# Operand tiles 64 bytes longer, read and written from 16 bytes past their start

## The chip, the cores and the metric

The kernel runs on one core of a Trainium2 chip. The metric is the device time of one execution in microseconds (us), the median of several runs; lower is better. A profile of one execution goes with it.

## What is computed

A two-layer encoder over 512 tokens of width 1024: layer 0 mixes tokens by neighbourhood attention (16 heads of 64), layer 1 by latent attention (low-rank queries and keys/values, 16 heads of 96). Each mixer's input projection also gives a SiLU gate; after each layer comes a sigmoid gate times an embedding projection.

```python
for i in range(DEPTH):                       # DEPTH = 2
    xn = rmsnorm(x, norm_g[i])
    if i % 2 == 0: y = mixer_na(xn, na_w_in[j], na_rpb[j], na_w_out[j])
    else:          y = mixer_mla(xn, mla_w_in[j], ..., mla_w_out[j])
    h = x + y
    gate = jax.nn.sigmoid(rmsnorm(h, ple_norm[i]) @ ple_w_gate[i])
    x = h + gate * (p[i] @ ple_w_proj[i])
return rmsnorm(x, final_norm)
# both mixers: (attention(...) * silu(z)) @ w_out
```

## The kernel before

Everything is float32 in memory. TensorE multiplies in a reduced float32 form (`float32r`), so each operand is kept as two tiles, a rounded part `hi` and the rest `lo`, and each product is the sum of three matmuls: hi by hi, lo by hi, hi by lo. A weight tile arrives by DMA in `wraw`; ScalarE copies it to `hi` (line 83, or 583 in the gate phases), and GpSimd, sometimes VectorE, subtracts to make `lo` (line 84 or 585). Activations are transposed on TensorE into PSUM and split the same way, by ScalarE (94) and VectorE (96), into "big" tiles of 128 partitions by four blocks of 512 elements.

The program runs through these stages: the layer-0 embedding projection and the first gates, the neighbourhood heads (projections at line 107, scores at 351 and 352, outputs at 400), the output projection, the gate matmul by seven block products (`gate_seven`, matmuls at 637), then the latent projections (`mla_c`), the latent heads (scores at 107, queries, keys and values at 734 and 107, outputs at 845), and the same tail again. A scheduler fixes the order of instructions on every engine when the program is built; `issue_after` pins some of them.

Two kinds of tile matter here. **Big tiles** come from `bigtile`, a pool of eight buffers of 8,192 bytes a partition; they hold the turned inputs (`x`, `x1`, `r`), the attention outputs (`o`, `o1`), the probabilities of the latent heads (`pt_hi`, `pt_lo`) and the blocks `X` of the gate matmul. **Weight tiles** `whi` and `wlo` (`w4` where more are kept) come from `load_w`, `gate_seven` and the start of `run`, mostly 4,096 bytes a partition. Not among them are the raw weights, the operands of the first embedding projection, the score operands of both kinds of head (`sa`, `da`, `qe`, `ke` and the like), the compressed latents `cT`, the values `vt` and the transposes' inputs.

In the built program before, all 2,916 matmuls on `float32r` read both operands from 32 bytes past a multiple of 64. The 488 transposes of data read the data from such a place too and the identity from a multiple of 64; the other 15 matmuls are the warm-up on a constant and four turns of a column of scales.

Of the kernel before, what the change touches and what calls it, by code (L numbers as in the profile page):

```python
# [13 lines left out]
F32 = mybir.dt.float32  # L14
F32R = mybir.dt.float32r
# [4 lines left out]
P = 128  # L20
S = 512
# [8 lines left out]
NLATE = 3  # L30
NEARLY = 7
SEVEN = (0, 1)


def win(t, r0, r1, off, dims):
# [5 lines left out]
class Trunk:  # L41
# [20 lines left out]
        self.sums = [{p: dram.tile([2 * P, D], F32, name=f"sum{l}{p}") for p in (4, 5, 6, 7)} for l in range(2)]  # L62

    def bigtile(self, name):
        return self.big.tile([P, 4, S], F32R, name=name, tag="big")

    def psum(self, tag, shape=(P, S)):
        t = self.ps.tile([P, S], F32, name="ps_" + tag, tag=tag, bufs={"mm": 2, "S": 2, "T": 3, "O": 1}[tag])
# [3 lines left out]
    def load_w(self, ap, n, extra=False, parts=1, rest=None, late=None):  # L72

        nc = self.nc
        pool = self.wx if extra else self.wp
        raw = self.wp.tile([P, 1024], F32, name="wraw", tag="wraw", bufs=3)
        tags = ("w4", "w4") if extra and self.wxn > 5 else ("whi", "wlo")
        hi, lo = (pool.tile([P, n if extra else 1024], F32R, name="whi"[:1] + t, tag=t, bufs=self.wxn if extra else 3)
                  for t in tags)
        w = n // parts  # L80
        for c in [slice(i * w, (i + 1) * w) for i in range(parts)]:
            self.last_load = nc.sync.dma_start(raw[:, c], ap[:, c])
            nc.scalar.activation(hi[:, c], raw[:, c], AF.Copy)  # L83
            f = lambda e, c=c: e.tensor_tensor(out=lo[:, c], in0=raw[:, c], in1=hi[:, c].bitcast(F32), op=ALU.subtract)  # L84
            if late is not None and c.stop == n:
                late.append(lambda: f(nc.gpsimd))
            else:
                f(rest or nc.gpsimd)
        return hi, lo
# [474 lines left out]
    def gate_seven(self, pool, layer, rh, res, after):  # L564
# [6 lines left out]
        def prep(p, after=None):  # L571
            nonlocal pieces
            W[p] = []
            src = self.quarter[layer][p] if p < 4 else self.sums[layer][p]
            for c in range(2):
                own = pieces % turns < 3
                pieces += 1
                raw = self.wp.tile([P, 1024], F32, name="wraw", tag="wraw", bufs=3)
                q, n = (self.wp, 3) if own else (pool, self.wxn)
                hi, lo = (q.tile([P, 1024], F32R, name=t, tag=t if own else "w4", bufs=n) for t in ("whi", "wlo"))  # L580
                nc.sync.dma_start(raw, src[c * P:(c + 1) * P])
                with self.tc.issue_after(after.ins) if after else nullcontext():
                    nc.scalar.activation(hi, raw, AF.Copy)  # L583
                for o in (slice(0, S), slice(S, 2 * S)):
                    nc.gpsimd.tensor_tensor(out=lo[:, o], in0=raw[:, o], in1=hi[:, o].bitcast(F32), op=ALU.subtract)  # L585
                W[p].append((hi, lo))
# [23 lines left out]
        for p in order[:4]:  # L610
            prep(p)
# [7 lines left out]
        for k, p in enumerate(order):  # L619
            if k in (1, 2):  # L620
                prep(order[k + 3])
# [5 lines left out]
            for i in range(2):  # L627
                for o, wd in halves if i and p in (7, 4) else ((0, S),):
# [26 lines left out]
                    elif p == 5:  # L655
                        q = self.psum("mm" if i else "T")
# [287 lines left out]
    def run(self):  # L944
        tc, nc, a = self.tc, self.nc, self.a
        def pair(n):
            return [self.bigtile(f"{n}h{g}") for g in range(2)], [self.bigtile(f"{n}l{g}") for g in range(2)]
# [4 lines left out]
        with tc.tile_pool(name="pre", bufs=4, reuse_waits="tile") as pool:  # L952
            ones = [nc.const_aps.tensor(1.0, (P, n), mybir.dt.bfloat16) for n in (P, S)]
            ps = self.psum("T")
            for i in range(NWARM):
                nc.tensor.matmul(ps, *ones, start=True, stop=True)
            operands = self.ple_load(0, pool)
            g0 = pool.tile([P, KD], F32, name="g0", bufs=1)
            nc.sync.dma_start(g0, a["g0"])

            raw, xT = pair("r"), pair("x")
            part = lambda T, k: [T[s][k // 4][:, k % 4, :] for s in range(2)]
            xs = [pool.tile([P, S], F32, name="xT", tag="xT", bufs=8) for k in range(KD)]
            ws = [[self.wp.tile([P, 1024], d, name=n, tag=n, bufs=3)
                   for n, d in (("wraw", F32), ("whi", F32R), ("wlo", F32R))] for _ in range(3)]
            first = ws.pop()
            for h in range(2):
                for k in range(4 * h, 4 * h + 4):
                    nc.sync.dma_start(xs[k], a["xT"][k])
                    hi, lo = part(raw, k)  # L970
                    nc.scalar.activation(hi, xs[k], AF.Copy, scale=g0[:, k:k + 1])
                    nc.vector.scalar_tensor_tensor(lo, xs[k], g0[:, k:k + 1], hi.bitcast(F32), op0=ALU.mult,
                                                   op1=ALU.subtract)
                for j in range(2):
                    wr, hi, lo = (x[:, h * S:(h + 1) * S] for x in ws[j])
                    nc.sync.dma_start(wr, a["na_z"][j][:, h * S:(h + 1) * S])
                    nc.scalar.activation(hi, wr, AF.Copy)
                    nc.vector.tensor_tensor(out=lo, in0=wr, in1=hi.bitcast(F32), op=ALU.subtract)
            ws = [w[1:] for w in ws]
            nc.sync.dma_start(self.ident, a["ident"])  # L980
            ss = pool.tile([P, NT], F32, name="ssq", bufs=1)
            xt = [pool.tile([P, D], F32, name="x", tag="x", bufs=4) for t in range(NT)]
            for t in range(NT):
                if t == 2:
                    nc.sync.dma_start(first[0], a["na_z"][2])
                nc.sync.dma_start(xt[t], a["x"][t])
                nc.scalar.activation(xt[t], xt[t], AF.Square, accum_out=ss[:, t:t + 1])
            self.ple(pool, 0, "pe", 6, operands)
            nc.gpsimd.tensor_scalar(ss, ss, 1.0 / D, EPS, op0=ALU.mult, op1=ALU.add)
            nc.gpsimd.tensor_scalar(self.rows[0][0], ss, 1.0, None, op0=ALU.add)  # L990
            nc.gpsimd.tensor_tensor(out=ss, in0=ss, in1=self.half.to_broadcast([P, NT]), op=ALU.pow)
            turned = self.transposes([ss[:, t:t + 1].to_broadcast([P, P]) for t in range(NT)])
            R = pool.tile([P, S], F32, name="R", bufs=1)
            nc.scalar.activation(first[1], first[0], AF.Copy)
            nc.gpsimd.tensor_tensor(out=first[2], in0=first[0], in1=first[1].bitcast(F32), op=ALU.subtract)
            nc.scalar.activation(R, turned, AF.Copy)
            zs = self.z_phase(a["na_z"], raw, range(2), R=R, ws=ws)
            for k in range(KD):
                hi, lo = part(xT, k)
                nc.vector.scalar_tensor_tensor(xs[k], turned, g0[:, k:k + 1], xs[k], op0=ALU.mult, op1=ALU.mult)  # L1000
                nc.scalar.activation(hi, xs[k], AF.Copy)
                (nc.vector, nc.gpsimd)[k % 2].tensor_tensor(out=lo, in0=xs[k], in1=hi.bitcast(F32), op=ALU.subtract)
            zs.update(self.z_phase(a["na_z"], raw, range(2, 8 - NLATE), R=R, first=first[1:]))
# [5 lines left out]
        for layer in range(2):  # L1009
            with tc.tile_pool(name=f"out{layer}", bufs=4, reuse_waits="tile") as pool:  # L1010
                seven = layer in SEVEN
                self.wx, self.wxn = pool, 10 if seven else 5
# [207 lines left out]
```

## Time and profile before

| | |
|---|---|
| median of 3 runs | 661.67 us (661.35 to 662.09) |
| the profiled execution | 660.85 us, of which its span is 658.7 us |
| TensorE matmuls | 647.8 us busy, 98% of the span |
| weight loads (beside the matmuls) | 550.8 us, 84% |
| VectorE, ScalarE, GpSimd | 61%, 67%, 66% of the span |
| granted TensorE clock, mean | 0.996 |

A matmul's "busy" time overlaps with the next one's, because matmuls are pipelined: one of 512 columns is shown as about 390 ns, while the next one starts some 227 ns later. So the pace is read from the chain of work that ended last, which gives the time that a run of matmuls took and how many they were, and not from the mean of one.

### The profile page before, as it was taken

Reading aid. Unit: us, or ns where it says so; the run is one execution under the profiler, and the core shown is the slowest. Engines: PE = TensorE matmul, PEld = TensorE weight load, DVE = VectorE, ACT = ScalarE, POOL = GpSimd, SP = SyncE. Lnnn points to the kernel's source line nnn. Section 1 sums busy time; section 2 is a strip of 40 time slices with the busy share of each in tenths; the row PEclk is TensorE's granted clock in tenths of the full one; section 3 lists DMA queues with packets and bytes.
Section 4 is the critical chain, followed back from the end, with each engine's and each line's share of the span. In section 5 each row is a group of like instructions: output and inputs, shape, how many; then the busy total and the mean of one; then the engine's idle time right before and its main releaser. Section 6 shows DMA issues by size and latency. Waiting matters only on the chain.

```text
span 658.7 us, 10121 instructions
## 1 busy us (share of the span) xinstructions
PE 647.8 (98%) x3419; PEld 550.8 (84%) x3419; DVE 403.7 (61%) x856; ACT 439.2 (67%) x875; POOL 432.8 (66%) x381
## 2 busy tenths in 40 slices
PE   9999999999999999999999999999999999999994
PEld 6888888988988888887899888888888888888884
DVE  6280365836646516568834613888888876474865
ACT  7672586757767743787543635887979897537945
POOL 0495485696686573787555525785959878436974
PEclk9999999999999999999999999999999999999998
DMA  9944256886577869445733334120111213583524
GB/s 328 346 149 142 97 169 186 231 203 160 166 212 175 223 166 348 158 149 162 247 85 118 103 102 148 54 77 6 63 53 65 66 65 128 200 312 128 168 89 159
DMA packets 44755, 102.18 MB, mean 155 GB/s; under 512 B 4640, under 2 KB 17696, under 8 KB 44704
## 3 DMA queue, kind: packets, MB, share of 16 engines
q1 hardware_dynamic: 33776, 83.97, 37.8%
q0 software_dynamic: 10496, 16.78, 11.7%
q10 hardware_dynamic: 432, 0.79, 0.3%
q8 instruction: 27, 0.44, 0.3%
q14 instruction: 24, 0.20, 0.1%
HBM read 89.99 MB, written 25.17 MB: 175 GB/s over the span
## 4 chain that ended last, share of the span: by engine, by line
PE 91%; DVE 2%; ACT 2%; POOL 2%; issue 1%; DMA 1%; POOLq 0%; ACTq 0%
PE ps_mm L107 35%; PE ps_S L107 13%; PE ps_mm L734 6%; PE ps_T L139 5%; PE ps_O L845 4%; PE ps_T L637 4%; PE ps_T L107 3%; PE ps_O L107 3%; PE ps_T L238 2%; PE ps_O L400 2%; PE ps_S L637 2%; PE ps_mm L637 2%; PE ps_mm L184 2%; PE ps_T L388 2%; PE ps_S L352 1%
## 5 line engine op out<-in xcount | busy, mean ns | idle before, releaser
L84 POOL TENSOR_TENSOR wwlo<-wraw,wwhi 128x1024 fp32r<-128x1024 f32 (+5 forms) x78 | 142.7, 1842 | 72.8 <-ACT wwhi L83 51.9
L83 ACT ACTIVATE wwhi<-wraw 128x1024 fp32r<-128x1024 f32 (+5 forms) x81 | 65.5, 832 | 54.5 <-issue 21.0
L585 POOL TENSOR_TENSOR wlo<-wraw,whi 128x512 fp32r<-128x512 f32 x56 | 73.9, 1352 | 24.2 <-ACT whi L583 19.3
L830 POOL TENSOR_TENSOR ex<-ex,rc 128x512 f32<-128x512 f32 x64 | 65.9, 1037 | 25.2 <-DVE rc L829 18.1
L828 ACT ACTIVATE ex<-ps_S,mx 128x512 f32<-128x512 f32 x64 | 44.0, 687 | 12.1 <-DVE mx L826 11.0
L826 DVE TENSOR_REDUCE mx<-ps_S 128x1 f32<-128x512 f32 x64 | 43.7, 682 | 7.1 <-PE ps_S L107 6.7
L96 DVE TENSOR_TENSOR pt_lo<-ps_T,pt_hi 128x512 fp32r<-128x512 f32 x64 | 43.3, 682 | 7.7 <-ACT pt_hi L94 7.3
L374 POOL TENSOR_TENSOR ex<-ex,rc 128x128 f32<-128x128 f32 (+1 forms) x64 | 35.7, 617 | 14.6 <-DVE rc L370 14.6
L94 ACT ACTIVATE pt_hi<-ps_T 128x512 fp32r<-128x512 f32 x64 | 37.7, 595 | 4.3 <-PE ps_T L139 4.1
L107 PE MATMUL ps_mm<-xh,wwhi 128*128 128x512 f32 x152 | 40.3, 398 | 0.0
L107 PE MATMUL ps_mm<-xl,wwhi 128*128 128x512 f32 x152 | 38.5, 391 | 0.0
L139 PE MATMUL ps_T<-ident,ex 128*128 128x128 f32 x256 | 38.4, 272 | 0.0
L107 PE MATMUL ps_mm<-xh,wwlo 128*128 128x512 f32 x152 | 38.2, 392 | 0.0
L139 PEld LDWEIGHTS ps_T<-ident,ex 128*128 128x128 f32 x256 | 31.5, 140 | 7.7 <-POOL ex L830 0.4
L107 PEld LDWEIGHTS ps_mm<-xh,wwlo 128*128 128x128 f32 x152 | 28.3, 188 | 5.9
L107 PEld LDWEIGHTS ps_mm<-xl,wwhi 128*128 128x128 f32 x152 | 28.4, 188 | 5.7
L583 ACT ACTIVATE whi<-wraw 128x1024 fp32r<-128x1024 f32 x28 | 29.2, 1055 | 5.1 <-DMA wraw<-sum 3.0
L205 DVE TENSOR_TENSOR u<-ps_O,u 64x512 f32<-64x512 f32 x32 | 22.0, 686 | 17.2 <-ACT u L204 16.7
L209 POOL TENSOR_TENSOR u<-u,z 128x512 f32<-128x512 f32 x16 | 21.8, 1360 | 16.0 <-DVE u L205 9.1
L368 ACT ACTIVATE ex<-ex,mx 128x128 f32<-128x128 f32 (+1 forms) x64 | 30.3, 475 | 1.9 <-DVE mx L358 1.1
L107 PEld LDWEIGHTS ps_mm<-xh,wwhi 128*128 128x128 f32 x152 | 27.3, 189 | 4.7
L107 PE MATMUL ps_S<-ke,qe 96*128 96x512 f32 x96 | 29.1, 408 | 0.3 <-DMA qe<-rl 0.3
(432 smaller groups left out, 1848.8 us busy)
## 6 DMA issues: line engine op xcount, KB each, us to landing
sum<-gate POOLq DMA_DIRECT2D x12, 1024.0 KB, 7.8
wraw<-na_qk SPq DMA_DIRECT2D x16, 512.0 KB, 3.3
wraw<-sum SPq DMA_DIRECT2D x16, 512.0 KB, 3.3
pe<-pe SPq DMA_DIRECT2D x31, 256.0 KB, 6.9
wraw<-gate SPq DMA_DIRECT2D x12, 512.0 KB, 3.4
wraw<-na_v SPq DMA_DIRECT2D x8, 512.0 KB, 4.2
sum<-sum POOLq DMA_DIRECT2D x4, 1024.0 KB, 9.0
wraw<-na_o SPq DMA_DIRECT2D x8, 512.0 KB, 3.6
```

What stands on the lines that cost most here:

```text
L83: nc.scalar.activation(hi[:, c], raw[:, c], AF.Copy)
L84: f = lambda e, c=c: e.tensor_tensor(out=lo[:, c], in0=raw[:, c], in1=hi[:, c].bitcast(F32), op=ALU.subtract)
L94: self.last_copy = nc.scalar.activation(hi, src, AF.Copy, scale=scale)
L96: nc.vector.tensor_tensor(out=lo, in0=src, in1=hi.bitcast(F32), op=ALU.subtract)
L107: last = self.last_mm = nc.tensor.matmul(out, l, r, start=i == 0, stop=i == n - 1)
L139: self.last_mm = self.nc.tensor.transpose(t[:, i * P:(i + 1) * P], b, self.ident)
L585: nc.gpsimd.tensor_tensor(out=lo[:, o], in0=raw[:, o], in1=hi[:, o].bitcast(F32), op=ALU.subtract)
L637: mm = nc.tensor.matmul(ps, l, r, start=j == 0 and p in banks, stop=j == 11 and p in (2, 3, 4), skip_group_check=True)
L734: self.last_mm = nc.tensor.matmul(PS[key], *terms[i], start=i == 0, stop=i == len(terms) - 1)
L826: nc.vector.reduce_max(mx, sp, axis=AX.X, negate=True)
L828: nc.scalar.activation(ex, sp, AF.Exp, bias=mx, accum_out=sm)
L830: nc.gpsimd.tensor_tensor(out=ex, in0=ex, in1=rc.to_broadcast([P, S]), op=ALU.mult)
```

## The change

Each of the tiles named above is allocated 16 elements (64 bytes) longer, and only the elements from the fifth on (16 bytes in) are used. `skewed` does both. It is called for big tiles, for the weight tiles of `load_w`, of `gate_seven` and of the start of `run`.

```diff
+GAP = 16
+BEGIN = 4
@@ bigtile
-        return self.big.tile([P, 4, S], F32R, name=name, tag="big")
+        return self.skewed(self.big, 4 * S, F32R, name, "big", 8).rearrange("p (a b) -> p a b", a=4)
+
+    def skewed(self, pool, n, d, name, tag, bufs, begin=BEGIN):
+        return pool.tile([P, n + GAP], d, name=name, tag=tag, bufs=bufs)[:, begin:begin + n]
@@ load_w
-        hi, lo = (pool.tile([P, n if extra else 1024], F32R, name="whi"[:1] + t, tag=t, bufs=self.wxn if extra else 3)
+        hi, lo = (self.skewed(pool, n if extra else 1024, F32R, "whi"[:1] + t, t, self.wxn if extra else 3)
                   for t in tags)
@@ gate_seven, prep
-                hi, lo = (q.tile([P, 1024], F32R, name=t, tag=t if own else "w4", bufs=n) for t in ("whi", "wlo"))
+                hi, lo = (self.skewed(q, 1024, F32R, t, t if own else "w4", n) for t in ("whi", "wlo"))
@@ run
-            ws = [[self.wp.tile([P, 1024], d, name=n, tag=n, bufs=3)
-                   for n, d in (("wraw", F32), ("whi", F32R), ("wlo", F32R))] for _ in range(3)]
+            ws = [[self.wp.tile([P, 1024], F32, name="wraw", tag="wraw", bufs=3),
+                   *(self.skewed(self.wp, 1024, F32R, n, n, 3) for n in ("whi", "wlo"))] for _ in range(3)]
```

In the built program the instructions of all five engines stand in the same order as before, with the same shapes. What differs is addresses. The tiles named start 48 bytes past a multiple of 64 where they started at 32. Before, all of them started at the same place of a stretch of 512 bytes (416); now neighbours in a pool differ by 64. Tiles behind these pools are pushed up by 64 bytes per buffer ahead of them and keep their place within 64. Of the 3,419 matmuls, 2,420 read at least one such tile: 1,892 of 512 columns, 336 of 256, 96 of 384 and 96 of 288. So do, reading or writing, 256 instructions of ScalarE, 159 of GpSimd and 125 of VectorE. Because buffers that were freed are covered by other tiles than before, ten instructions wait for other semaphores (four on VectorE, one on ScalarE, five DMAs of SyncE); one of them, a VectorE subtraction of the second output projection, now also waits for GpSimd, and two VectorE multiplies there no longer do.

## The prediction

> **What bounds the kernel now.** I read the page's busy times first, then its chain of work that ended last, then that chain in order of time, for the pace of single stretches.
>
> ```profile
> span 658.7 us, 10121 instructions
> PE 647.8 (98%) x3419; PEld 550.8 (84%) x3419; DVE 403.7 (61%) x856; ACT 439.2 (67%) x875; POOL 432.8 (66%) x381
> PEclk9999999999999999999999999999999999999998
> PE 91%; DVE 2%; ACT 2%; POOL 2%; issue 1%; DMA 1%; POOLq 0%; ACTq 0%
> ```
>
> TensorE (PE) holds 91% of the chain, and its clock is granted in full nearly everywhere. The other three engines together hold 6%, about 40 us. So this change pays or costs almost only through the pace of matmuls; what it does to ScalarE, VectorE and GpSimd counts in those 40 us alone. The chain in order of time (start, us, what) gives the pace of runs of one shape:
>
> ```profile
> 66.15 16.32 PE ps_mm L107 x72
> 333.88 4.87 PE ps_S L107 x28
> 343.94 4.24 PE ps_T L107 x32
> 425.67 0.93 PE ps_O L845 x4
> 438.97 1.44 PE ps_mm L107 x12
> ```
>
> The first run is projections of 512 columns: 16.32 / 72 = 226.7 ns each. The second is latent projections of 384 columns: 173.9 ns. The third is the same of 288 columns: 132.5. The fourth is latent-head outputs of 512 columns: 232.5. The fifth is values of 256 columns: 120. From 256 to 512 columns the pace grows by 106.7 ns, 0.417 ns a column, which leaves 226.7 - 512 x 0.417 = **13.3 ns a matmul that is not columns**. At 384 columns the same split gives 160 + 13.9, and at 288 it gives 120 + 12.5. That is the quantity at stake: a fixed piece of each matmul, present at every width, for which no engine is waited for.
>
> **Is that piece made by other engines' traffic to the tiles?** Within the first stretch the columns of the next view are: the stretch, its us, busy us of PE, weight loads, VectorE, ScalarE and GpSimd with their counts, granted clock, DMA share.
>
> ```profile
> 66.15:82.47 16.32, 16.32 (x75) 13.52 (x74) 5.87 (x14) 8.99 (x16) 7.18 (x3) 1.00 0.29 97
> 400.00:560.00 160.00, 159.67 (x867) 133.78 (x866) 129.42 (x257) 133.32 (x292) 126.91 (x116) 1.00 0.22 68
> ```
>
> In the first, GpSimd (7.18 us) and ScalarE (8.99) work for about half of the time, mostly on `lo` and `hi` tiles, and the pace is 226.7. Two later runs of the same projections, in the middle of the neighbourhood heads:
>
> ```profile
> 139.24 10.91 PE ps_mm L107 x48
> 151.27 5.49 PE ps_mm L107 x24
> ```
>
> They take 227.3 and 228.8. So what the other engines do around a projection adds a nanosecond or two, not thirteen. In the latent heads, where three engines are busy for 80% of the time, matmuls of 512 columns take about 232.5, 5.8 more; but the engines there mostly read the matmuls' own results in PSUM, which the change doesn't move.
>
> **The change, part by part.** No instruction is added, removed or moved, and no transfer grows: the raw weights land in tiles of the same size. So there are four terms.
>
> *The start of matmul operands.* 2,420 matmuls (of the built program: 1,892 of 512 columns, 336 of 256, 96 of 384, 96 of 288) read at least one tile from 16 bytes further on. Nothing in the trace has a float32r operand that starts at 48 past 64, so this has no row of its own, and I bound it. From below, the whole fixed piece goes: 2,420 x 13.3 ns = 32 us off. From above, it doubles: 32 us on. Between them, one more unit to fetch per matmul would cost what its columns cost: 16 bytes are 4 columns, 1.7 ns, in all 4 us; 32 bytes are 8 columns, 3.3 ns, 8 us. The nearest rows are the five paces. Their tiles lie at many different places beyond 512 bytes, and the 288-column weights alternate between two places within 512 (their rows are 1,152 bytes); the piece stays at 12.5 to 13.9. That looks like a price of changing weights, not of the address. I take **0**.
>
> *Neighbouring tiles no longer in step.* Before, all tiles started at one place of 512 bytes, so a collision between a weight load and the running matmul, if there is one, would be alike everywhere. Now it would vary from pair to pair. Since 384 and 512 columns pay the same piece, although the weight load is long over when the longer one ends, I take 0 here too, with the same bounds as above, not to be added to them.
>
> *Work of the other engines on these tiles.* The costliest groups, with busy us and mean ns of one:
>
> ```profile
> L84 POOL TENSOR_TENSOR wwlo<-wraw,wwhi 128x1024 fp32r<-128x1024 f32 x41 | 100.3, 2454 | 51.1 <-ACT wwhi L83 35.8 <-PE ps_O L238 7.5 <-PE ps_mm L107 7.1
> L84 POOL TENSOR_TENSOR wwlo<-wraw,wwhi 128x1024 fp32r<-128x1024 f32 x3 | 7.2, 2394 | 9.1 <-PE ps_mm L107 6.1 <-PE ps_O L238 3.1
> L84 POOL TENSOR_TENSOR ww<-wraw,ww 128x1024 fp32r<-128x1024 f32 x4 | 10.5, 2613 | 12.0 <-ACT ww L83 12.0
> L83 ACT ACTIVATE wwhi<-wraw 128x1024 fp32r<-128x1024 f32 x43 | 45.1, 1058 | 40.9 <-issue 21.0 <-PE ps_O L238 8.8 <-DMA wraw<-na_z 4.3
> L83 ACT ACTIVATE ww<-wraw 128x1024 fp32r<-128x1024 f32 x10 | 10.1, 1051 | 12.6 <-DMA wraw<-mla_o 7.1 <-DMA wraw<-na_o 5.5
> ```
>
> The second row is the quiet stretch from 66 us. The same subtraction takes 2,394 to 2,613 ns from place to place, a band of 9%; the copy 1,051 to 1,058. GpSimd's share of the chain is 2%, 13 us; 9% of it is 1.2 us. ScalarE's and VectorE's 13 us each, at the copy's band of 1%, give 0.1. Most of this work lies beside matmuls: in the first stretch GpSimd is idle for 9 of 16 us. If a subtraction were late, the matmul that reads `lo` would wait, the last third of each product; the place with no cover is the turn from output projection to gate matmul:
>
> ```profile
> 282.59 3.00 POOL wlo L585 x2
> 285.61 3.28 DMA wraw<-sum
> 288.99 1.06 ACT whi L583
> ```
>
> There 9% of 3.00 is 0.3 us. I take 0, bounds minus 1.3 and plus 1.3.
>
> *Ten changed waits.* The one that adds an engine is a VectorE subtraction of the second output projection that now follows GpSimd; queued behind it on VectorE are the sums of that projection, which the turns of `hg` and so TensorE wait for. At worst it waits out one subtraction, 2.6 us by the row above; the two multiplies that lose a wait on GpSimd could win as much. The five SyncE moves of the rotary slab keep their order and trade waits among themselves, so the last of them can go at about the same time. I take 0, bounds plus and minus 2.6.
>
> **The sum** is 0 + 0 + 0 + 0 on the profiled execution's 660.85 us (span 658.7 and 2.15 around it). The three shown runs have their median 0.8 above it, so I predict **661.7 us**. The small terms alone give plus or minus 3.9, 658 to 666.
>
> **The Trainium skill against the rows.** "SBUF — State Buffer", Specifications (TRN2), states lines of 16 bytes. By that rule a start 16 bytes on is at the start of a line again and nothing changes, which agrees with my sum; the trace has no case that tests it. "TensorE: Matmul & The Clock Gate", Back-to-back issue gap, gives columns / 2.4 plus 2.5 ns for warm matmuls, an estimate of 215.8 ns at 512 columns. The row above says 226.7, so the measurement decides on the pace; but if the 10.8 ns between them were a price of where these tiles start, they could be won: 2,420 x 10.8 = 26 us, 636 us. No run here shows which it is. It speaks for the first rival below.
>
> **The rivals.**
>
> *Operands read faster from the new places.* Part of the 13.3 ns then is a stall that comes from all tiles starting in step, or 32 past 64. For it: the piece is there at every width, with no engine waited for. Against: it doesn't vary over the many places that the trace has. Half of it would be 16 us, 646 us; all of it 630.
>
> *Operands read slower, one more unit per matmul.* A start 32 past 64 is a multiple of 32; 48 is not. If operands come in units of 32 bytes, each of the 2,420 matmuls fetches one more. The price is 8 columns each, 8 us: 670 us, on the other side from no change. It decides from about 0.6 ns a matmul (1.3 us, 0.2%). Since matmuls run back to back through 91% of the chain, nothing would hide it. Against: no row shows such a unit.
>
> *Slower by the small terms.* GpSimd's subtraction at the top of its band and the added wait: 1.3 + 2.6 = 3.9, and as likely half of it: 664 us. Faster by the same terms: 659.
>
> *The change does nothing at all* is my forecast itself, since all it does is move addresses.
>
> **How the numbers follow.** No change 0.30. Matmuls faster 0.28, the small terms faster 0.07. Matmuls slower 0.22, the small terms slower 0.13. This kernel's runs differ by 0.1%, so about 0.2% (1.3 us) can be told from no change. That makes faster 0.35, same 0.30, slower 0.35. The likeliest case's own range is 658 to 666. For 8 in 10 the range must reach into both matmul cases: down to 644, just past half of the fixed piece (what is left out below is some 0.10), up to 672, one unit of 32 bytes with the small term (some 0.10 above).
>
> **What would show it.** In the profile after, the stretch of 72 projections should still take 16.3 us, the 384-column run 4.9 and the 288-column run 4.2; the GpSimd subtraction of 1,024 should stay between 2,394 and 2,613 ns. If the 72 take 16.6 or more, the second rival holds; if 15.8 or less, the first. If the runs keep their pace and the time still moves, the waits or the stretch from 276 to 306 us have changed. The forecast is wrong if the pace of 512 columns moves by more than 0.6 ns.

## The result, and the profile after

The kernel with the change takes 666.9 us (666.57 to 668.54, 4 runs) against 661.69 us before (661.35 to 662.09, 4 runs). The ratio is 1.008, with a 95% interval of 1.0065 to 1.0094: slower by 0.8%, 5.2 us. The profiled execution's span is 664.8 us, 6.1 more than before. The page of the kernel after, its span, busy times, granted clock and shares of the chain:

```profile
span 664.8 us, 10122 instructions
...
PE 653.5 (98%) x3419; PEld 550.9 (83%) x3419; DVE 403.5 (61%) x856; ACT 439.1 (66%) x875; POOL 434.2 (65%) x381
...
PEclk9999999999999999999999999999999999999998
```

TensorE is busy for 5.7 us longer, of the 6.1 that the span grew; the clock is as before, and so, within 0.3%, are the other three engines. Now the chain in order of time (start, us, what), the same runs of matmuls as in the prediction:

```profile
67.19 16.63 PE ps_mm L112 x72
...
141.16 11.12 PE ps_mm L112 x48
...
337.30 4.92 PE ps_S L112 x28
...
347.43 4.23 PE ps_T L112 x32
...
439.85 0.93 PE ps_O L850 x4
...
443.53 1.42 PE ps_mm L112 x12
```

The 72 projections went from 16.32 to 16.63 us, from 226.7 to 231.0 ns each; the 48 from 227.3 to 231.7; the 384-column run from 173.9 to 175.7; the 288-column run from 132.5 to 132.2. The latent outputs stayed at 0.93 and the 256-column values lost 0.02 us. So the price lies in the wide projections and gates. There are 1,608 matmuls of 512 columns with both operands in moved tiles; at the 3.5 ns or so that they lost each (231.0 against 227.5, from the starts of successive matmuls in the two traces) they make 5.6 us, close to the 5.7 that TensorE lost.

Is it traffic of other engines? The same stretch of 72, by engine (busy us of PE, weight loads, VectorE, ScalarE, GpSimd, then clock and DMA share), and GpSimd's subtraction:

```profile
67.19:83.82 16.63, 16.63 (x74) 13.53 (x74) 5.80 (x13) 9.00 (x16) 7.28 (x3) 1.00 0.29 96
```

```profile
L89 POOL TENSOR_TENSOR wwlo<-wraw,wwhi 128x1024 fp32r<-128x1024 f32 x41 | 100.9, 2468 | 52.7 <-ACT wwhi L88 36.7 <-PE ps_O L243 7.8 <-PE ps_mm L112 7.3
L88 ACT ACTIVATE wwhi<-wraw 128x1024 fp32r<-128x1024 f32 x43 | 45.1, 1058 | 42.2 <-issue 22.4 <-PE ps_O L243 8.9 <-DMA wraw<-na_z 4.3
```

The others do the same work for the same time, the subtraction takes 2,468 ns against 2,454, the copy 1,058 as before. The matmuls themselves are slower with nothing new beside them. In the trace after, the mean of matmuls of 512 columns with no other engine at work is 231.0 ns (110 of them), and 230.8 with all three at work for the whole time (272); before, it was 226.9 and 228.1. Matmuls with nothing beside them lost 4 ns: the loss is TensorE's own.

The stretch between output projection and gate matmul, where other engines set the time, shows the two subtractions at 3.00 us before and this after:

```profile
285.80 3.01 POOL wlo L590 x2
288.83 3.12 DMA wraw<-sum
```

### The profile page after: what moved, and what is told of

It reads as the page before. It is cut to its first block, busy times and chain, and to the rows that moved or that the text cites. A ratio compares the mean times of both kernels' runs of the same rounds, so it can differ in the third digit from the quotient of the medians.

```text
span 664.8 us, 10122 instructions
## 1 busy us (share of the span) xinstructions
PE 653.5 (98%) x3419; PEld 550.9 (83%) x3419; DVE 403.5 (61%) x856; ACT 439.1 (66%) x875; POOL 434.2 (65%) x381
## 4 chain that ended last, share of the span: by engine, by line
PE 88%; DVE 3%; DMA 3%; POOL 2%; issue 2%; ACT 2%; POOLq 0%; DVEq 0%; ACTq 0%
PE ps_mm L112 34%; PE ps_S L112 13%; PE ps_mm L739 6%; PE ps_T L144 5%; PE ps_T L642 4%; PE ps_O L850 4%; PE ps_T L112 3%; PE ps_O L112 3%; PE ps_T L243 2%; PE ps_S L642 2%; PE ps_O L405 2%; PE ps_mm L189 2%; PE ps_mm L642 2%; PE ps_T L393 1%; DMA sum<-gate 1%
```

## The experiments

All kernels below do the whole computation. "Distance" is how far apart the two operands of one matmul start, taken within 256 bytes, whichever of the two comes first: 64 and 192 are both called 64. Paces of 512 columns in the text are means of the time from one matmul's start to the next one's, from the trace of each run, for projections, gates and the first embedding; a matmul whose next one starts more than 14 ns late is left out, and the latent heads are not in them.

**First question: is it where a tile starts, or how the tiles stand to each other?** The change does two things, the 16 bytes at the start and the 64 bytes between neighbours.

gap_only, the longer tiles used from their first element:

```diff
-BEGIN = 4
+BEGIN = 0
```

> Tiles 64 bytes longer, used from their first element (start 32 past 64 as before). Theory START (the place of an operand's start within 64 bytes sets the cost): pace of 512-column projections back at 227 ns, time 661.7 us. Theory STEP (neighbours no longer at one place of 512 bytes): pace stays at 231 ns, time 667 us.

667.6 us, ratio 1.0093 (1.0078 to 1.0108). The pace is 231.3 ns. The start is back where it was and nothing is won: STEP.

begin8, tiles start at a multiple of 64 bytes:

```diff
-BEGIN = 4
+BEGIN = 8
```

> Used from the ninth element, so tiles start at a multiple of 64 bytes. START with a unit of 32 bytes: pace 227 ns, 661.7 us. START with a unit of 64 bytes: faster than before, pace 223 or less, 655 us or less. STEP: pace 231 ns, 667 us.

667.57 us, ratio 1.0097 (1.0081 to 1.0112). STEP again: no unit of 32 or of 64 bytes shows. The chain in order of time, the 72 projections of gap_only and of begin8:

```profile
67.32 16.66 PE ps_mm L112 x72
```

```profile
67.56 16.66 PE ps_mm L112 x72
```

16.66 / 72 is 231.4 ns a matmul in both, against 231.0 after the change: three kernels that begin their tiles in three different places, at one price.

big_only and weights_only give the change to one kind of tile (the other kind is allocated as before):

```diff
 def bigtile(self, name):        # weights_only
-        return self.skewed(self.big, 4 * S, F32R, name, "big", 8).rearrange("p (a b) -> p a b", a=4)
+        return self.big.tile([P, 4, S], F32R, name=name, tag="big")
```

> Only big tiles get the 64 bytes and start 16 bytes in; weight tiles are as before. START, moving side alone counts: matmuls with a big tile moving at 231 ns, those with weights moving at 227; 768 x 3.5 ns = 2.7 us, time 664.4 us. START, either side counts: both kinds at 229 to 231, 664 to 667 us. STEP: both kinds between 227 and 231.

> Only weight tiles are changed. START, moving side alone counts: matmuls with weights moving at 231 ns, those with a big tile moving at 227; 792 x 3.5 ns = 2.8 us, time 664.5 us. START, either side counts: both kinds at 229 to 231, 664 to 667 us. STEP: both kinds between 227 and 231.

big_only takes 668.78 us, ratio 1.0114 (1.0099 to 1.0129), weights_only 667.6, 1.0101 (1.0079 to 1.0122). Either half alone costs at least as much as both together. That fits no price per tile or per moved start; it fits a price on pairs, since each half alone puts more pairs out of step: of 2,132 `float32r` matmuls of 512 columns, 1,688 have a distance other than 0 in big_only and 1,884 in weights_only, but 1,482 after the change. STEP itself had put the pace of both halves between 227 and 231; it was 232.0 in big_only and 231.8 in weights_only, so that part was missed. The count alone doesn't explain why big_only, with fewer such pairs, takes longer than weights_only.

**Second question: the place, or the distance?** shift64, shift32 and shift256 are the kernel before with an unused constant ahead of all other tiles, so that every tile moves and all distances stay 0:

```diff
+        pad = self.const.tile([P, 16], F32, name="pad")   # 8 and 64 in the others
+        nc.gpsimd.memset(pad, 0.0)
         self.ident = self.const.tile([P, P], F32, name="ident")
```

> The kernel before, with an unused constant of 64 bytes a partition ahead of all other tiles: every tile is moved by 64 bytes and all stay in step, multiples of 512 bytes apart. STEP (what counts is how the tiles of one matmul stand to each other): pace 227 ns, 661.5 us. PLACE (what counts is the place itself within 512 bytes, and 416 happened to be a good one): pace 229 to 232 ns, 664 to 669 us.

> As shift64 with 32 bytes: all tiles start at a multiple of 64 bytes, in step. STEP: pace 227 ns, 661.5 us. PLACE: 229 to 232 ns, 664 to 669 us. A unit of 64 bytes, if there is one: below 227 ns, under 659 us.

> As shift64 with 256 bytes. STEP: pace 227 ns, 661.5 us. PLACE: 229 to 232 ns, 664 to 669 us.

661.23 us, ratio 0.9993 (0.9979 to 1.0008); 661.15, 0.9992 (0.998 to 1.0003); 661.37, 0.9996 (0.9983 to 1.0009). The pace is 227.4 ns in all three. The place doesn't matter, and a start at a multiple of 64 bytes (shift32) wins nothing.

weights256 makes only the six working weight tiles longer, by 256 bytes (the weights kept for the output projections and gates are as before, here and in the four kernels that follow):

```diff
-GAP = 16
-BEGIN = 4
+GAP = 64
+BEGIN = 0
@@ skewed (bigtile, left out here, is as before)
+        gap = GAP if pool is self.wp else 0
-        return pool.tile([P, n + GAP], d, name=name, tag=tag, bufs=bufs)[:, begin:begin + n]
+        return pool.tile([P, n + gap], d, name=name, tag=tag, bufs=bufs)[:, begin:begin + n]
```

> The six working weight tiles alone are 256 bytes longer, used from their first element; big tiles and the kept weights of the output projections are as before. So weights stand 0 or 256 past the activations within 512 bytes. STEP by steps of 64 or 128 bytes alone: pace 227 ns, 661.5 us. STEP by any distance that is not a multiple of 512: those three of six weight tiles that are off by 256 at 231 ns, the others at 227, some 664 us.

661.47 us, ratio 0.9998 (0.9986 to 1.0011). Longer tiles and slices of them cost nothing by themselves, and 256 bytes out of step cost nothing: the 491 matmuls that run while weights 256 out of step within 512 are loaded go at 227.4 ns, like the rest.

**Third question: does each pair count for itself, and which distances hurt?** The next three are weights256 with another `BEGIN`, so that all working weights stand at one constant distance from the activations: 16, 64 and 128 bytes. The tiles outside the working pool start at their first element.

```diff
-BEGIN = 0
+BEGIN = 4       # 16 and 32 in the others
```

> As weights256, but the six working weight tiles are used from their fifth element: every one stands 16 bytes past the activations within 256, alike for all. 1,302 matmuls of 512 columns have such a weight tile. PAIR (the distance within 256 bytes between the two operands of a matmul counts): those 1,302 at 231 ns, some 666 us. SPREAD (that distances change from tile to tile counts, a constant distance is harmless): 227 ns, 661.5 us.

> The same from the seventeenth element: every working weight tile 64 bytes past the activations within 256. PAIR: the 1,302 at 231 ns, some 666 us. SPREAD: 227 ns, 661.5 us. PAIR with the line of 16 bytes alone (16 hurts, 64 doesn't): 661.5 us here and 666 in weights256_b4.

> The same from the thirty-third element: every working weight tile 128 bytes past the activations within 256. PAIR with a period of 256 bytes: 231 to 233 ns, 666 to 668 us. PAIR with a period of 128, or SPREAD: 227 ns, 661.5 us.

> The six working weight tiles are 128 bytes longer, used from their first element: half of them stand 0 and half 128 past the activations within 256; 602 matmuls of 512 columns have the distance 128. PAIR with a period of 256: those 602 at 231 to 233 ns, the rest at 227, some 664 us. PAIR with a period of 128: 661.5 us. SPREAD: all projections at 230 or more, 665 to 667 us.

| distance of the changed pairs | us | ratio (95%) | pace at this distance | pace at distance 0, same run |
|---|---|---|---|---|
| 16, constant | 666.57 | 1.008 (1.0065 to 1.0095) | 231.6 | 228.2 |
| 64, constant | 667.56 | 1.0096 (1.0081 to 1.0111) | 232.6 | 228.2 |
| 128, constant | 667.96 | 1.0101 (1.0086 to 1.0116) | 232.1 | 228.1 |
| 0 and 128 (weights128: `GAP = 32`, `BEGIN = 0`) | 665.32 | 1.0066 (1.005 to 1.0083) | 231.7 | 228.4 |

PAIR, with a period of 256 bytes: SPREAD had put the three constant distances at 661.5 us. A constant distance costs as much as a spread one, and within one run the pairs left at distance 0 keep nearly the old pace. The chain of weights256_b16 in order of time shows both: the rows that start at 85.33, 141.82 and 408.53 are projections with working weights, those at 261.61 and 274.98 half and whole products of the output projection with kept weights.

```profile
85.33 5.60 PE ps_mm L113 x24
...
141.82 11.20 PE ps_mm L113 x48
...
261.61 2.72 PE ps_O L113 x12
...
274.98 5.51 PE ps_T L113 x24
...
408.53 5.60 PE ps_mm L113 x24
```

5.60 / 24 and 11.20 / 48 are 233.3 ns, which is 6.7 more than 226.7; 2.72 / 12 is 226.7, as before the change, and 5.51 / 24 is 229.6 where it was 228.8 (5.49, in a row of the chain before).

At 16 bytes there is no one pace. The chain of weights256_b4:

```profile
16.78 10.88 PE ps_mm L190 x48
...
39.19 5.60 PE ps_mm L113 x24
...
44.79 1.39 PE ps_T L244 x6
...
67.02 16.34 PE ps_mm L113 x72
...
84.32 5.60 PE ps_mm L113 x24
```

All five have the distance 16. Two run at 226.7 and 226.9 ns, two at 233.3, and the row of six, the first of twelve like it, at 231.7. So a distance that isn't a multiple of 256 allows a slow pace; at 16 it doesn't force it. What chooses in a given stretch is open.

What the distance does shows when the starts are taken by place in a stream, that is, in a row of `float32r` matmuls of 512 columns that each start less than 242 ns after the one before (a pause or another width ends it; means in ns, the latent heads left out):

| place in the stream | before, all at distance 0 | weights256_b16, streams all at distance 64 |
|---|---|---|
| 1 and 2 | 232.8 | 233.4 |
| 3 to 6 | 230.0 | 233.2 |
| 7 to 12 | 227.1 | 233.2 |
| 13 and on | 226.7 | 233.3 |

Both start slow. In step, the stream settles at the fast pace within a dozen matmuls; one that is wholly 64 bytes out of step doesn't. Stretches at 64 bytes in streams that hold pairs at distance 0 as well can lie between (46 matmuls from 574.97 us in weights256_b16 at 229.3). So a pair doesn't count quite for itself: what stands before it in the stream counts too. That fits pairs at distance 0 coming out at 230.4 to 230.8 in gap_only and after the change, where they lie among others. In gap_only, 376 of 439 are among the first six in a row at distance 0, and the mean falls from 231.2 for the first two to 226.9 from the thirteenth on. Whether it is a matmul's own weights that count, or those of the next one, loaded while it runs, the runs don't part: the two mostly stand at the same distance.

## Why the prediction was right and wrong

**What bounds the kernel: right.** Of the 6.1 us by which the span grew, 5.7 went through the pace of matmuls, which was named as the one thing that could move the time. The stretch of 72 at 16.63 us is just over the 16.6 that was given as the sign of slower matmuls.

**The forecast of no change: wrong.** The time moved by 5.2 us, four times what was to count as no change, though the range of 644 to 672 holds it. The term that failed is the second of the four, "neighbouring tiles no longer in step", taken as 0 and measured at 5.7 us of TensorE's time.

**The first term, the start of operands: 0 was right.** begin8, gap_only and the shifts say so. The 16-byte lines of the Trainium skill quoted there ("SBUF — State Buffer", Specifications (TRN2)) agree with those runs as far as starts go; that row says nothing of two operands, and the conclusion "nothing changes" did not follow from it.

**The reasons given.** The second term was taken as 0 because 384 and 512 columns pay the same fixed piece, and the first because that piece is alike over "many different places". Both were read from pairs in step: in the program before, every matmul of 384 and of 512 columns has its operands a multiple of 256 bytes apart, so no row of these widths could show what leaving that costs. Out of step the two widths part: 384 columns lost 1.8 ns, 512 columns some 3.5. The one exception among the `float32r` matmuls was in the prediction's own words: the 288-column weights, whose rows of 1,152 bytes put every other one 128 bytes off. Behind the row of 32 that the prediction read, the chain before has this one:

```profile
348.70 2.08 PE ps_T L107 x16
```

Its mean is 130.0 ns, but by the starts in that trace its pairs at distance 0 take 128 to 129 ns and those at 128 bytes 131 to 132, in turn. The hint was there, hidden in a mean.

**What the other engines do: over-read.** The prediction took the 227.3 and 228.8 ns of two later rows for a nanosecond or two of their doing. By place in the stream that is the slow start: in the trace before, matmuls from the thirteenth on take 226.8 ns with the three engines at work nearly all the time (211 of them) and 226.9 with them nearly idle (130). The 232.5 of the latent heads, set beside their busy engines, comes in short groups between transposes. Their streams settle later than the others (231.3 in places 7 to 12, 228.0 from the thirteenth on), and why is open.

**"Operands read slower, one more unit per matmul": right in sign and nearly in size, wrong in mechanism.** It gave 3.3 ns and 670 us; measured were 3.5 ns on the widest matmuls and 666.9. But a start at a multiple of 32 or 64 bytes costs as much as one at 16, so there is no such unit; the two sizes only happen to be alike. The range reached up to 672 because of this unit, so that it holds the time is in part luck. A forecast that had been settled by the size alone would have carried the wrong rule away.

**"Operands read faster": excluded for what was tried.** The long streams of the five kernels in step settle at 226.7, and the mean pace of the nine kernels out of step is higher than that of those in step, so the fixed 13.3 ns is no price of the starts tried here. The 10.8 ns above the estimate of 215.8 can't be won by them either. The Trainium skill ("TensorE: Matmul & The Clock Gate", Back-to-back issue gap) gives the formula behind that estimate for a matmul's gap in isolation, not for a stream of weight loads and matmuls, and this stream stays above it in every run. What the 13.3 ns are was not tried.

**The small terms: right to leave out.** GpSimd's subtraction moved by 14 ns of 2,454, and 0.01 us on the path; the rest of the span's growth outside matmuls is 0.4 us, in which the ten changed waits must lie. The waits alone were not tried.

## What to carry to other kernels

When TensorE is the bound, compare where the two operands of a matmul start relative to each other, not only where each starts: here streams of 512 columns with operands multiples of 256 bytes apart settled at 226.7 ns, and whole rows of the chain with them 16, 64 or 128 bytes apart ran at up to 233.3. Tiles of round sizes behind each other had this for nothing, and padding them apart by other sizes broke it; if padding is needed for something else, 256 bytes cost nothing here. And a mean pace over a run of alternating pairs hides exactly the difference that such a change makes: split it, by pair and by place in the stream, before calling it constant.

## What the runs showed of the hardware

The pace of a stream of matmuls of 512 columns, each with a weight load of its own, depends on the distance between the starts of the moving and the stationary operand within 256 bytes. At distance 0 a stream starts at 232.8 ns and settles at 226.7 within a dozen matmuls; a stream wholly at 64 bytes stays at 233.2 to 233.4, and stretches at 64 bytes in mixed streams can run at 229.3; at 16 bytes some streams settle and others run at 231.7 or 233.3. The 231 ns after the change are a mixture of distances. The other engines don't set the settled pace (226.8 ns beside them, 226.9 without). With 256 columns the same distances cost nothing (1.42 us for 12, against 1.44). That weight load and moving stream meet in some part of the memory is a guess that fits and isn't shown; the runs show the distance, not the circuit.
